# The second attention layer's first head: values turned to token rows by transposing transfers instead of TensorE transposes

## The chip, the cores and the metric

The kernel runs on one core of a Trainium2 chip. The metric is the device time of one execution in microseconds (us), as the median of several runs. Engines are named as the profile names them: PE is TensorE's matmul, PEld its weight load, DVE VectorE, ACT ScalarE, POOL GpSimd, SP the engine that issues most transfers. Each engine takes its instructions strictly in the order of its queue.

## What is computed

A two-layer trunk over 528 tokens (16 learned meta tokens and 512 real ones), width 1024, in float32. Layer one is gated linear attention; layer two is differential softmax attention with 8 heads:

```python
def diff_branch(xn, w_in, lam_vecs, gnorm, w_out, rel_table, lambda_init):
    proj = xn @ w_in
    q, k, v, z = jnp.split(proj, 4, axis=-1)          # per head: 2x128 q, 2x128 k, 256 v, 256 z
    ...
        s = jnp.einsum('bhpqd,bhpkd->bhpqk', qb, kh) * scale + bias[None, :, None]
        s = jnp.where(dist >= 0, s, -jnp.inf)
        p = jax.nn.softmax(s, axis=-1)
        a = p[:, :, 0] - lam * p[:, :, 1]
        return jnp.einsum('bhqk,bhkv->bhqv', a, vh)
    ...
    o = head_rms(o) * gnorm.astype(f32) * (1.0 - lambda_init)
    y = jax.nn.silu(z.astype(f32)) * o.reshape(B, L, D_INNER)
    return (y.astype(xn.dtype) @ w_out)
```

A final RMSNorm follows and the meta positions are dropped. What matters here: the value projection `v` comes out with channels on the partitions and tokens along the free axis, and the product of the attention weights with `v` needs tokens on the partitions. So `v` of every head has to be turned.

## The kernel before

**Precision.** Each float32 operand is split into a high and a low part (`split`: ACT writes the rounded high part, DVE subtracts it and writes the low one), and a product takes three matmul passes. Weights arrive by SP in `raw` (two buffers of 1 MB), ACT and DVE split them into `wh`/`wl`, `a11h`/`a11l` and so on, and PE consumes these. Most projections run as a `Unit`: a block product with seven instead of eight sub-products (p1 to p7), whose weight sums (`sum`, `raw<-raw,sum`, L360) are made by DVE. A unit's first product leaves its result in the PSUM bank `bx`; ACT copies it out (`partial`, L446, tile `u`), and only then may p6 add to the same bank.

**Order.** PE's order is the order in which the program issues its instructions. For the layer's steps a `Weaver` decides it: `fill` interleaves projection work with attention steps by estimated microseconds, `defer` runs a function after so much work, `follow` does the same for chains of steps. DVE, ACT and the transfers are placed by the framework's scheduler, with priorities (`urgent`, `soon`); after that each queue is fixed.

**Around the change.** At the end of layer one the program projects z and then v of head 0 of layer two (`z0r` in tile `x6`, `v0` in tile `x5`, stored back to front so that real tokens run from 511 down to 0 and the meta tokens from 15 to 0 stand in the last 16 columns). Then come, in this order on PE, q of head 0 (L415, banks `bv` and `by`), k of head 0 (L415, `bx` pair, then `bv`/`by`), the z projection of head 1 as a unit (L425, p1 in `bx`, p2 in `by`, p6 in `bx`), and inside it the first scores (L394). Beside this DVE and ACT make the sums of x that the units need (`token_sums2`, L1515 and the splits of `x4` to `x7`), split q and k, and split weights.

**How v is turned before.** `turned_back2(s, m, vt, first=True)` is called for m = 0 and 1. Each defers `post`: four 128x128 TensorE transposes into one PSUM bank (L856) and one of the last 32 columns (L857), then the splits into `s.v` (two tiles, tokens x 4 blocks x 256 channels) and `s.vm` (the meta tokens).

**How v of heads 1 to 6 is turned.** `turn_by_dma`: `leave` (called for each half m) has ACT rearrange the 32-bit words into two planes of 16-bit words (L583, tile `planes`) and issue a transfer to a DRAM buffer `vd` (L584). When both halves have left, `turn` is put on the list `behind` and issued on SP right after the next weight load: two transposing transfers into `planes` (L592) and one of 128 rows into `lands` for the meta tokens (L594). Later `done` splits `planes` into `s.v` (ACT L569, DVE L570) and `rest` splits the meta rows out of `lands` (L401, L402, L406). `tick` is a small DVE memset that keeps `done` behind a chosen instruction.

## Time and profile before

| | before |
|---|---|
| runs, us | 981.64, 981.70, 983.57; median 981.70 |
| the profiled execution, us | 980.58 |
| its span (first to last instruction), us | 978.8 |
| PE busy | 965.6 us, 99% of the span |
| DVE busy | 777.6 us, 79% |
| ACT busy | 621.5 us, 63% |
| mean granted TensorE clock | 0.999 of full speed |
| value splits of heads 1 to 6 from `planes` | L569 and L570, 12 instructions each |

Times in the trace are us from the span's start. "SPq" and "ACTq" rows are issues of transfers, not engine work. A matmul's row covers its pipeline, so neighbouring matmuls overlap; the distance between starts is what each costs. The stretch that the change touches lies between 478 us (end of v0's projection) and 530 us, in a program of 979 us.

### The profile page before, as it was taken

The page shows a single profiled execution, that of the slowest core. Times are in us where ns is not written, and L with a number is a line of the kernel's source. Part 1 is how long each engine was busy: PE and PEld are TensorE (multiplying, and loading weights), DVE is VectorE, ACT ScalarE, POOL GpSimd, SP SyncE. Part 2 cuts the span into 40 slices and gives each one's busy share as a digit, 9 for nine tenths or more (in the row PEclk, how much of TensorE's full clock was granted, in tenths as well). Part 3 has the DMA queues.
Part 4 walks back from the last instruction along what each step waited for, and adds up shares of the span by engine and source line. Part 5 has one row for each costly group of instructions (what it writes and reads, how often), then busy time and mean ns, then how long its engine had stood idle before and what let it go on. Part 6 is the DMA issues. An engine that isn't in the chain of part 4 may idle for free.

```text
span 978.8 us, 18153 instructions
## 1 busy us (share of the span) xinstructions
PE 965.6 (99%) x7049; PEld 913.2 (93%) x7049; DVE 777.6 (79%) x1584; ACT 621.5 (63%) x1310; POOL 50.3 (5%) x68
## 2 busy tenths in 40 slices
PE   9999999999999999999999999999999999999997
PEld 8999999999999999998999998899998999989996
DVE  7889885887888797566997985977968879677785
ACT  8775755567647556545757774576764667655573
POOL 1000000000000100000001001001010000000001
PEclk9999999999999999999999999999999999999999
DMA  7322224625363122212323424134252351612212
GB/s 195 87 85 62 77 72 136 146 94 130 120 153 114 59 87 87 72 59 87 98 87 95 139 75 148 54 98 137 86 147 86 94 141 47 186 57 86 87 65 86
DMA packets 113226, 98.37 MB, mean 100 GB/s; under 512 B 37341, under 2 KB 99069, under 8 KB 113136
## 3 DMA queue, kind: packets, MB, share of 16 engines
q1 hardware_dynamic: 109680, 90.66, 32.1%
q10 hardware_dynamic: 3456, 6.51, 1.9%
q8 instruction: 57, 0.93, 0.4%
q14 instruction: 33, 0.27, 0.1%
HBM read 83.64 MB, written 8.62 MB: 94 GB/s over the span
## 4 chain that ended last, share of the span: by engine, by line
PE 88%; DVE 2%; ACT 1%; issue 0%; POOLq 0%; ACTq 0%
PE bx L425 19%; PE bv L425 12%; PE bx L415 10%; PE by L425 10%; PE ps L394 9%; PE bx L962 5%; PE bx L394 3%; PE bv L962 2%; PE by L962 2%; PE by L394 2%; PE bv L394 2%; PE ps L1200 2%; PE by L415 1%; PE bv L415 1%; PE ps L1792 1%; PE bx L1792 1%
## 5 line engine op out<-in xcount | busy, mean ns | idle before, releaser
L274 DVE TENSOR_TENSOR wl<-raw,wh 128x1024 fp32r<-128x1024 f32 x98 | 119.6, 1222 | 23.4 <-ACT wh L273 16.2
L273 ACT ACTIVATE wh<-raw 128x1024 fp32r<-128x1024 f32 x98 | 103.1, 1054 | 53.5 <-PE by L962 24.7
L425 PE MATMUL bv<-x,wh 128*128 128x264 f32 (+1 forms) x656 | 97.9, 287 | 0.6 <-DVE z L473 0.6
L425 PE MATMUL bx<-x,wh 128*128 128x264 f32 (+1 forms) x640 | 95.2, 286 | 1.8 <-ACT u L446 1.5
L425 PEld LDWEIGHTS bv<-x,wh 128*128 128x128 f32 x656 | 86.4, 189 | 1.5 <-DVE z L473 0.9
L425 PEld LDWEIGHTS bx<-x,wh 128*128 128x128 f32 x640 | 84.5, 188 | 3.2 <-ACT u L446 2.4
L446 ACT ACTIVATE u<-bx 128x264 f32<-128x264 f32 (+1 forms) x120 | 45.5, 380 | 28.1 <-PE bx L425 24.4
L415 PE MATMUL bx<-x,wh 128*128 128x512 f32 (+1 forms) x256 | 62.6, 386 | 0.0
L274 DVE TENSOR_TENSOR wl<-sum,wh 128x1024 fp32r<-128x1024 f32 x41 | 50.1, 1222 | 15.2 <-ACT wh L273 14.6
L1715 POOL TENSOR_TENSOR st<-st,mhalf 128x1 f32<-128x1 f32 x32 | 31.5, 984 | 465.4 <-ACT on L1713 447.1
L425 PE MATMUL bv<-x,wl 128*128 128x264 f32 (+1 forms) x328 | 55.2, 285 | 0.1
L425 PE MATMUL bx<-x,wl 128*128 128x264 f32 (+1 forms) x320 | 54.0, 285 | 0.0
L1679 ACT ACTIVATE p<-p,st 128x528 f32<-128x528 f32 (+3 forms) x64 | 36.4, 569 | 24.6 <-DVE st L1677 24.1
L415 PEld LDWEIGHTS bx<-x,wh 128*128 128x128 f32 x256 | 44.5, 188 | 8.0
L273 ACT ACTIVATE wh<-sum 128x1024 fp32r<-128x1024 f32 x41 | 43.3, 1055 | 9.5 <-PE bv L425 3.4
L273 ACT ACTIVATE a11h<-raw 128x512 fp32r<-128x512 f32 x41 | 25.7, 628 | 35.5 <-DMA raw<-in_diff_w_in_dram 16.0
L425 PE MATMUL by<-x,a12h 128*128 128x264 f32 (+1 forms) x320 | 46.5, 285 | 0.0
L425 PE MATMUL bx<-x,a11h 128*128 128x264 f32 (+1 forms) x320 | 46.3, 285 | 0.0
L425 PEld LDWEIGHTS bv<-x,wl 128*128 128x128 f32 x328 | 45.9, 188 | 0.4 <-issue 0.3
L425 PEld LDWEIGHTS bx<-x,wl 128*128 128x128 f32 x320 | 45.2, 188 | 0.8 <-DVE wl L274 0.5
L425 PEld LDWEIGHTS bx<-x,a11h 128*128 128x128 f32 x320 | 42.2, 188 | 0.7
L425 PEld LDWEIGHTS by<-x,a12h 128*128 128x128 f32 x320 | 41.7, 188 | 0.0
(483 smaller groups left out, 2641.7 us busy)
## 6 DMA issues: line engine op xcount, KB each, us to landing
raw<-in_gla_w_in_dram SPq DMA_DIRECT2D x48, 512.0 KB, 4.1
raw<-in_diff_w_in_dram SPq DMA_DIRECT2D x42, 512.0 KB, 4.2
raw<-in_diff_w_in_dram SPq DMA_DIRECT2D x11, 1024.0 KB, 5.8
raw<-in_gla_w_out_dram SPq DMA_DIRECT2D x8, 1024.0 KB, 5.1
raw<-in_diff_w_out_dram SPq DMA_DIRECT2D x8, 1024.0 KB, 5.9
vd<-planes ACTq DMA_DIRECT2D x12, 268.0 KB, 2.5
vd<-keep ACTq DMA_DIRECT2D x8, 264.0 KB, 2.6
T<-bdr SPq DMA_DIRECT2D x8, 264.0 KB, 3.5
```

The lines of the kernel that those rows point to most:

```text
L273: act.activation(hi, src, AF.Copy)
L274: dve.tensor_tensor(lo, src, hi.bitcast(F32), op=ALU.subtract)
L394: pe.matmul(ps, l, r, start=first and n == 0, stop=last and n == 2, **kw)
L415: pe.matmul(bank, a[:, k, :], b[k] if n0 is None else b[k][:, n0 + i * nn:n0 + (i + 1) * nn], start=n == 0 and ks[0] == 0, stop=n == len(t ...
L425: pe.matmul(bank[:, :x[q].shape[2]], w[p][:, k * P:(k + 1) * P], x[q][:, k, :], start=first and i == 0, stop=i == len(PASSES) - 1, skip_gr ...
L446: W.moved = act.activation(t, self.bx[:, :self.n], AF.Copy, scale=self.sc)
L962: pe.matmul(banks[i][:, :HT], h.t[p][:, k, mm * P:(mm + 1) * P], s.y[q][k][:, i * HT:(i + 1) * HT], start=n == 0, stop=n == len(PASSES) - 1)
L1200: pe.matmul(o, s.kd[:, i, kc], s.qs[:, i, t0:t0 + n], start=i == 0, stop=i == 1)
L1679: act.activation(p[:, :nk], p[:, :nk], AF.Exp, scale=-1.0, bias=st[:, m:m + 1], accum_out=st[:, 2 + m:3 + m])
L1715: pool.tensor_tensor(ms, ms, mhalf[:, :1], op=ALU.pow)
L1792: pe.matmul(ps[i], yp[hd][p][:, k, b * P:(b + 1) * P], wt[q][cs.start // 512][:, 2 * hd + k, cs.start % 512:(cs.stop - 1) % 512 + 1], star ...
```

## The change

Head 0's values now take the road of heads 1 to 6. The call for m = 0 makes a `turn_by_dma` object with its own `planes` tile of 2 x 528 words; both calls `leave` at once. Two arguments are new: `ahead` (how much work lies between the second `leave` and the appearance of `turn` on the list; 3.0 instead of 4.0) and `at` (which rows of `lands` hold the meta tokens: row 96, since here the last 128 columns are read and the meta tokens come last).

```diff
-    def turn_by_dma(planes, groups, ends, us, done, last):
+    def turn_by_dma(planes, groups, ends, us, done, last, at=0, ahead=4.0):
...
-                W.follow((4.0, lambda: behind.append((turn, None))))
+                W.follow((ahead, lambda: behind.append((turn, None))))
...
-                last(lands[0][:32, 0, :])
+                last(lands[0][at:at + 32, 0, :])
...
-        if first or s is heads[-1]:
-            W.defer(2.2 if first else 1.4, post)
+        if s is heads[-1]:
+            W.defer(1.4, post)
+        elif first:
+            if m == 0:
+                s.leave = turn_by_dma(T(ep, [P, 2, L], F32, "planes", bufs=1),
+                                      [(slice(3, 1, -1), 0), (slice(1, None, -1), 2 * P)], L - P, 3.0, done, last, 96, 3.0)
+            s.leave(m, vt)
```

On PE the ten transposes (two times L856 x4 and L857) between the 12th and the 13th matmul of q's first half are gone, and nothing else in its order differs. On SP the three transposing transfers stand behind the two loads of `raw_1571`, the weights of head 1's z unit, and ahead of the next two loads. DVE gets the small memset of `tick` earlier, ahead of v0's projection. Otherwise ACT's and DVE's queues differ only from the end of v0's projection to about 527 us of the trace before, in head 0's second turn of the attention weights; behind that they are the same as before. Buffer numbers at the end of names differ between the two programs; the first number tells the tile.

ACT, first place: from the high parts of q and of the x sums (`x4` to `x7`) to those of head 1's z weights (`a11h`, `a12h`, `a22h`). Before:

```order
L273 ACTIVATE v0_1536_8777<-ps_1548_8817 128x4x128
L273 ACTIVATE x4_1551_8833<-hT_8_90 128x4x8
L273 ACTIVATE wh_1556_8854<-raw_1555_8852 128x1024
L273 ACTIVATE a11h_1573_9033<-raw_1571_9027 128x512
L276 ACTIVATE q0_1558_8858<-bv_1540_8782 128x512
L273 ACTIVATE a12h_1578_9045<-raw_1571_9027 128x512
L273 ACTIVATE a22h_1582_9054<-raw_1571_9027 128x512
```

Now, the same place further on in the queue:

```order
L276 ACTIVATE q0_1557_8844<-by_1559_8848 128x512
L569 ACTIVATE v0_1536_8777<-planes_1539_8780,tick_1560_8868 128x4x128 x2
L401 ACTIVATE vm_1538_8779<-lands_1554_8838,short_146 32x256
L402 ACTIVATE vm_1538_8779<-lands_1554_8838,short_146 32x256
L273 ACTIVATE x6_1551_8817<-hT_8_90 128x4x8
L273 ACTIVATE x7_1552_8818<-hT_8_90 128x4x256
L273 ACTIVATE a11h_1573_9028<-raw_1571_9022 128x512
L273 ACTIVATE a12h_1578_9040<-raw_1571_9022 128x512
L273 ACTIVATE a22h_1582_9049<-raw_1571_9022 128x512
```

The value splits moved from the front of q's splits to behind the second of them, and `x7` and the three weight splits now stand behind the value splits.

ACT, second place: the end of k's projection (`t`, `k0`) and the copy `u` out of `bx` in head 1's z unit. Before:

```order
L1643 ACTIVATE t_1566_8900<-by_1570_8966 128x264
L273 ACTIVATE wh_1580_9050<-raw_1571_9027 128x1024
L273 ACTIVATE k0_1563_8897<-t_1566_8900 128x512
L446 ACTIVATE u_1589_9082<-bx_1585_9061 128x256
L273 ACTIVATE k0_1563_8897<-t_1566_8900 128x16
```

Now:

```order
L1648 ACTIVATE t_1566_8890<-by_1570_8961 128x264
L273 ACTIVATE k0_1563_8887<-t_1566_8890 128x512
L273 ACTIVATE k0_1563_8887<-t_1566_8890 128x16
L273 ACTIVATE wh_1580_9045<-raw_1571_9022 128x1024
L446 ACTIVATE u_1589_9077<-bx_1585_9056 128x256
```

The weight split `wh_1580`, which reads the last weight sum that DVE makes in `raw_1571`, was two rows ahead of `u` and is now right ahead of it, behind k's splits.

DVE: from the low part of q's second half to the last weight sum (`raw<-raw,sum`). Before, the rows right behind q's second half:

```order
L277 SCALAR_TENSOR_TENSOR q1_1559_8859<-by_1560_8862,q0_1558_8858 128x512
L277 SCALAR_TENSOR_TENSOR x5_1552_8834<-hT_8_90,x5_1552_8834 128x4x256
L277 SCALAR_TENSOR_TENSOR x5_1552_8834<-hT_8_90,x5_1552_8834 128x4x8
L274 TENSOR_TENSOR x6_1553_8835<-hT_8_90,x6_1553_8835 128x4x8
L1515 TENSOR_TENSOR hT_8_90<-hT_8_90 128x4x256
L1515 TENSOR_TENSOR hT_8_90<-hT_8_90 128x4x8
L360 TENSOR_TENSOR sum_1575_9037<-raw_1571_9027 128x512
```

Now:

```order
L277 SCALAR_TENSOR_TENSOR q1_1558_8845<-by_1559_8848,q0_1557_8844 128x512
L570 TENSOR_TENSOR v1_1537_8778<-planes_1539_8780,v0_1536_8777 128x4x128
L277 SCALAR_TENSOR_TENSOR x5_1550_8816<-hT_8_90,x5_1550_8816 128x4x8
L570 TENSOR_TENSOR v1_1537_8778<-planes_1539_8780,v0_1536_8777 128x4x128
L406 SCALAR_TENSOR_TENSOR vm_1538_8779<-lands_1554_8838,short_146,vm_1538_8779 32x256
L274 TENSOR_TENSOR x6_1551_8817<-hT_8_90,x6_1551_8817 128x4x256
L274 TENSOR_TENSOR x6_1551_8817<-hT_8_90,x6_1551_8817 128x4x8
L1515 TENSOR_TENSOR hT_8_90<-hT_8_90 128x4x8
L274 TENSOR_TENSOR x7_1552_8818<-hT_8_90,x7_1552_8818 128x4x256
L274 TENSOR_TENSOR x7_1552_8818<-hT_8_90,x7_1552_8818 128x4x8
L274 TENSOR_TENSOR a11l_1574_9029<-raw_1571_9022,a11h_1573_9028 128x512
```

The three value instructions moved from ahead of q's first half to behind its second half; `x6`, `a11l` moved from ahead of them to behind them, and `x5`'s large part and one large L1515 moved to ahead of q's second half.

## The prediction

> **What bounds the kernel now.** I read the page's busy times and its chain first, then the chain of waits in order of time and the busy times by windows around the change, and last the timelines of each engine there.

> ```profile
> PE 965.6 (99%) x7049; PEld 913.2 (93%) x7049; DVE 777.6 (79%) x1584; ACT 621.5 (63%) x1310; POOL 50.3 (5%) x68
> PE 88%; DVE 2%; ACT 1%; issue 0%; POOLq 0%; ACTq 0%
> ```

> TensorE is busy for 99% of the span and 88% of the chain that ended last is TensorE's. The chain in order of time shows what the transposes cost on it:

> ```profile
> 478.25 2.78 PE bv L415 x12
> 481.03 0.44 PE ps L856 x4
> 481.57 0.44 PE ps L856 x4
> 482.12 2.79 PE bv L415 x12
> 484.91 5.61 PE by L415 x24
> ```

> q's first half (`bv`, 24 matmuls) takes from 478.25 to 484.91, 6.66 us, with the transposes inside; its second half (`by`, the same 24) takes 5.61. The ten transposes thus cost **1.05 us of the chain**. What stands beside TensorE there, by windows:

> ```profile
> core 0: us, PE busy (x) PEld busy (x) DVE busy (x) ACT busy (x) POOL busy (x), PEclk, DMA share, GB/s
> 480.00:490.00 10.00, 10.00 (x50) 8.20 (x49) 9.73 (x18) 8.84 (x18) 0.00 (x0) 1.00 0.40 122
> 490.00:500.00 10.00, 10.00 (x83) 9.91 (x82) 10.00 (x17) 5.00 (x12) 0.00 (x0) 1.00 0.34 107
> 500.00:510.00 10.00, 10.00 (x87) 10.00 (x85) 9.68 (x23) 5.85 (x14) 0.00 (x0) 1.00 0.32 105
> 486.00:492.00 6.00, 6.00 (x34) 5.14 (x33) 6.00 (x9) 4.61 (x8) 0.00 (x0) 1.00 0.00 0
> ```

> The reader is to see three things: TensorE has no hole here that the change could close beyond its own transposes; DVE has no room either (9.7 to 10 of 10 us), so whatever makes DVE wait comes out later; ACT has about 5 us of room in 490 to 500, and from 486 to 492 no transfer runs (share 0.00).

> **The change, part by part.** *Removed from PE:* the 1.05 us. It is all on the chain; without a new wait the end comes 1.05 us earlier.

> *ACT and DVE work.* The durations of the same steps for later heads:

> ```profile
> L583 ACT ACTIVATE planes<-t x12: 1079/1082/1098, 529.4 to 839.3; 128x1072 uint16<-128x1072 uint16 x12
> L569 ACT ACTIVATE v<-planes,tick x12: 707/710/727, 558.3 to 878.7; 128x512 fp32r<-128x512 f32 x12
> L570 DVE TENSOR_TENSOR v<-planes,v x12: 677/685/689, 560.3 to 881.9; 128x512 fp32r<-128x512 f32 x12
> L406 DVE SCALAR_TENSOR_TENSOR vm<-lands,short,vm x1: 474/474/474, 561.7 to 561.7; 32x256 fp32r<-32x256 f32 x1
> DMA to landing us min/median/max: 2.3/2.5/2.8
> ```

> ACT gains two rearrangements of 1.08 us; its splits change from PSUM to `planes` at about the same price. So some 2 us more on ACT, inside its room. DVE trades splits for splits (0.69 us each), a wash. The work itself costs nothing; what can cost is the waiting of ACT and DVE in order behind the transfers.

> *When the transfers land.* ACT's and SP's rows before:

> ```profile
> 479.35 1.32 ACT L1557 ACTIVATE x<-x,dgs 128x512 f32<-128x512 f32 x2
> 480.25 0.92 SPq L295 DMA_DIRECT2D raw<-in_diff_w_in_dram  x2
> 492.21 0.92 SPq L295 DMA_DIRECT2D raw<-in_diff_w_in_dram  x2
> ```

> By the new order ACT does the two rearrangements where L1557 stood (479.35 to 481.4), then L1557, and issues both transfers to `vd` at about 482.1 to 482.5. They need 2.3 to 2.8 us (last row of the fence above), and the weight load issued at 480.25 is moving at the same time (until about 485, since the share is 0.00 from 486). I take `vd` landed at 485 to 486.5. SP waits for that, then issues the transposing transfers; behind them in SP's queue stands only the load that was issued at 492.21, so it isn't held back. How long they take, from another head with little beside them:

> ```profile
> 719.90 2.59 SPq L592 DMA_TRANSPOSE planes<-vd  x2
> 722.54 1.25 SPq L594 DMA_TRANSPOSE lands<-vd  x1
> 721.00:722.50 1.50, 1.50 (x14) 1.50 (x14) 1.11 (x3) 1.50 (x5) 0.00 (x0) 1.00 0.81 167
> 722.50:723.00 0.50, 0.50 (x4) 0.40 (x3) 0.41 (x2) 0.47 (x4) 0.00 (x0) 1.00 0.54 62
> 723.00:724.50 1.50, 1.50 (x8) 1.18 (x7) 1.50 (x3) 0.69 (x3) 1.27 (x1) 1.00 1.03 180
> 724.50:725.00 0.50, 0.50 (x4) 0.40 (x3) 0.26 (x1) 0.40 (x2) 0.06 (x1) 1.00 0.59 56
> ```

> Two bursts with a dip after each: the second of the two ends some 4.7 us after the first issue; with the signal I take 5. So `planes` is there at **490 to 491.5**, `lands` a good microsecond later.

> *When the queues reach the value splits.* ACT stands before L569 once q's second half is split; q's last matmul ends at 490.52 - 1.05 = 489.5 (the chain's `by` row: 484.91 + 5.61), so ACT is there at about 490.2. DVE's rows:

> ```profile
> 492.10 0.68 DVE L277 SCALAR_TENSOR_TENSOR q<-by,q 128x512 fp32r<-128x512 f32 x1
> 492.70 1.32 DVE L277 SCALAR_TENSOR_TENSOR x<-hT,x 128x1024 fp32r<-128x1024 f32 x2
> 495.27 0.68 DVE L360 TENSOR_TENSOR sum<-raw 128x512 f32<-128x512 f32 x1
> 495.87 0.68 DVE L274 TENSOR_TENSOR a12l<-raw,a12h 128x512 fp32r<-128x512 f32 x1
> 501.41 0.69 DVE L360 TENSOR_TENSOR raw<-raw,sum 128x512 f32<-128x512 f32 x1
> ```

> A 512-wide step costs DVE 0.60 us (495.27 to 495.87), a 1024-wide one 1.14 by the same reckoning. DVE left q's second half at 492.7; ahead of that point the new order has one 512-wide split, two value splits and one meta pair less (2.4 us) and 1.14 us more of x sums; it waits 0.6 us for the later L1557, where before 0.27 us of 480 to 490 were idle (9.73 of 10), so 0.3 more. It gets to L570 at about **491.7**, or 0.7 us after ACT's L569 starts if that is later: with `planes` at 490 to 491.5, at 491.7 to 492.2.

> *Who waits for that.* Behind L570 on DVE stand `x6`, `x7`, `a11l`, k's low part and all weight sums down to `raw<-raw,sum`. That last row came 9.35 us after q's split (492.70 to the end of 501.41's step, 502.05). In the new order the stretch from L570 to it has two value splits (1.2), the meta rows (0.45), `x6` (1.14) and `a11l` (0.60) more, and `x5` and one L1515 (1.14 each) less: 10.4 us. I add 0.3 for ACT's meta rows, which DVE meets. DVE is through at 502.4 to 502.9. Then ACT:

> ```profile
> 502.68 1.07 ACT L273 ACTIVATE wh<-raw 128x1024 fp32r<-128x1024 f32 x1
> 503.63 0.63 ACT L273 ACTIVATE k<-t 128x512 fp32r<-128x512 f32 x1
> 504.15 0.39 ACT L446 ACTIVATE u<-bx 128x256 f32<-128x256 f32 x1
> 504.87 0.87 PE L425 MATMUL bx<-x,wh 128*128 128x256 f32 x6
> 521.61 1.57 PE L394 MATMUL ps<-v,aT 128*128 128x256 f32 x12
> ```

> In the new order `wh` (0.95 as a step) waits for that sum and `u` (0.39) stands right behind it; PE's p6 (504.87) may not add to `bx` before `u` is out. `u` ends at 502.4 + 0.95 + 0.4 = 503.8 to 504.3. PE, 1.05 us early, wants p6 at 503.8. Before, `u` ended at 504.54, 0.33 us ahead of p6. So p6 is **late by 0 to 0.5 us**, and from there each microsecond of delay at L570 is one on the chain. The other waits have more room: the values themselves are needed only at 521.61, `a11h` about 6 us after it is made; k's low part has about 1 us.

> *Sum.* Gain 1.05 minus 0.25 (middle of 0 to 0.5) = 0.8 us. The profiled execution took 980.58 (span 978.8), so its counterpart would take 979.8; the median of the runs is 1.1 us above that execution, so the median goes from 981.7 to **980.9**. From the second turn of head 0's attention weights on the orders agree, so nothing else moves.

> [...] The trace has nobody wait for the values before 521.61, which is why I weigh the queues' wait and not the transfers' length.

> **The rivals.** 0.2% is 1.96 us here, about what a measurement of this kernel can tell from no change.

> *1, the forecast: gain kept, less at most 0.5 us;* 980.65 to 981.2. For it: no transfer runs from 486 to 492, and TensorE has no other wait. Chance 0.53; of this 0.06 would be read as over 0.2% faster, by the scatter of the runs alone (981.64 to 983.57).

> *2, gain eaten.* `planes` at 491.5 to 494: p6 is late by 0.5 to 3 us, and the time is 981.2 to 983.6, in the middle 982. For it: where a load was issued right ahead, the pair's issue alone took longer:

> ```profile
> 536.46 4.28 SPq L592 DMA_TRANSPOSE planes<-vd  x2
> 843.92 6.04 SPq L592 DMA_TRANSPOSE planes<-vd  x2
> ```

> That is 1.7 us more than 2.59, so `planes` at 492.5 and p6 1.3 us late. Against it: these had their load half a microsecond ahead, here it is 5 us. Chance 0.32, of it 0.03 over 0.2%.

> *3, slower: DVE and ACT stand in front of the transfers.* If `vd` is held to 486.5 by the weight load and the pair is as slow as at 843.92 (3.45 us more), `planes` comes at 495, DVE starts L570 at 495.7, and p6 is 4 us late: 981.7 - 1.05 + 4 = 984.6. It decides from `planes` at 494 on (3 us lost, 1.05 won). [...] Chance 0.15, of it 0.12 over 0.2%.

> A gain over 1.96 us would need holes in TensorE that the windows don't show. That the transfers aren't used is out: the order has them, and the transposes are gone.

> **How the numbers follow.** The time is rival 1's, 980.9. The range 980.0 to 983.4 holds rivals 1 and 2 and leaves 0.2 out: scatter below (0.06) and rival 3 above with the end of rival 2. Faster 0.06; slower 0.03 + 0.12 = 0.15; within 0.2% the rest, 0.79.

> **What would show it.** Right: q's two halves both 5.6 us; `planes` split by ACT at 490 to 491.5 with little idle time before; `raw<-raw,sum` at about 502; `u` ending within 0.5 us of p6's start. Wrong: idle time of ACT ahead of L569 and of DVE ahead of L570 above 1.5 us with L1515, x sums and k's low part pushed out, and PE waiting for ACT's `u` (L446) or for DVE's k ahead of the scores (L394); or a PE hole behind 505 that has another releaser.

## The result, and the profile after

The changed kernel takes 987.62 us in the median (986.93 to 987.80), the kernel before, timed beside it, 981.64; the ratio is 1.0059, 95% interval 1.0047 to 1.007. It is some 6 us slower. The forecast was 980.9 with a range to 983.4, so it was wrong in size and in sign. The profiled execution took 987.65 us with a span of 985.6, 6.8 more than the span before; 0.65 of this is there ahead of the change (q starts at 478.74 instead of 478.09).

The page's busy times; TensorE does 10 matmuls fewer and idles more:

```profile
span 985.6 us, 18136 instructions
PE 966.0 (98%) x7039; PEld 912.3 (93%) x7039; DVE 777.4 (79%) x1584; ACT 623.8 (63%) x1310; POOL 51.8 (5%) x68
```

TensorE's timeline from q to the first scores (start, duration, what, and in brackets the idle time before it and who ended it):

```profile
478.74 3.87 PE L415 MATMUL bv<-x,wh 128*128 128x512 f32 x16
...
484.30 3.90 PE L415 MATMUL by<-x,wh 128*128 128x512 f32 x16
...
502.53 0.63 PE L425 MATMUL bx<-x,a11l 128*128 128x256 f32 x4
504.99 1.40 PE L425 MATMUL by<-x,a12h 128*128 128x256 f32 x8 [1.83 <-ACT t L1648]
506.19 1.05 PE L425 MATMUL by<-x,a12l 128*128 128x256 f32 x4
507.65 1.65 PE L425 MATMUL bx<-x,wh 128*128 128x256 f32 x6 [0.41 <-ACT u L446]
509.10 1.68 PE L394 MATMUL ps<-k,q 128*128 128x264 f32 x12
```

The kernel before has its first scores here:

```profile
505.58 1.61 PE L394 MATMUL ps<-k,q 128*128 128x264 f32 x12
```

q's first half takes 5.56 us instead of 6.66: the gain is there, 1.1 us. Then TensorE stands still twice, 1.83 and 0.41 us, and the matmuls behind the first stand are slow: p6 takes 1.65 us where it took 0.87. Against the kernel before TensorE was 0.45 us early at 482 us and is 3.52 us late at the scores (509.10 against 505.58), so this stretch costs 3.97 us. From the start of q's first half to the scores it is 30.36 us instead of 27.49, a net loss of 2.87. The windows over it (the column behind POOL is the granted clock):

```profile
504.00:506.00 2.00, 1.01 (x8) 1.01 (x9) 2.00 (x3) 1.67 (x5) 0.00 (x0) 0.96 0.00 0
506.00:508.00 2.00, 1.59 (x7) 1.30 (x7) 1.97 (x6) 1.73 (x3) 0.00 (x0) 0.50 0.00 0
508.00:510.00 2.00, 2.00 (x13) 2.00 (x13) 1.98 (x4) 0.64 (x2) 0.00 (x0) 0.69 0.05 9
```

The clock is halved from about 505.8 to 509.2: 2 us times (0.04 + 0.50 + 0.31) are 1.70 us of full speed lost. The two stands are 2.24 us; together 3.94. The sum fits, but its terms aren't independent prices: p6 may start only when `u` is out, at 507.60 (last ACT row below), however fast the matmuls ahead of it run. Section 7 has an execution without this fall of the clock in which the scores come as late.

Why TensorE stands: the timelines of SyncE's queue, of ScalarE and its queue (ACTq), and of VectorE.

```profile
480.90 0.92 SPq L295 DMA_DIRECT2D raw<-in_diff_w_in_dram  x2
488.63 2.61 SPq L592 DMA_TRANSPOSE planes<-vd  x2
...
482.07 0.82 ACTq L584 DMA_DIRECT2D vd<-planes  x2
...
494.18 1.34 ACT L569 ACTIVATE v<-planes,tick 128x512 fp32r<-128x512 f32 x2 [3.33 <-DMA planes<-vd]
...
503.32 1.06 ACT L273 ACTIVATE wh<-sum 128x1024 fp32r<-128x1024 f32 x1 [2.55 <-DVE sum L360]
...
504.55 0.38 ACT L1648 ACTIVATE t<-by 128x264 f32<-128x264 f32 x1
...
507.24 0.36 ACT L446 ACTIVATE u<-bx 128x256 f32<-128x256 f32 x1
...
494.93 0.69 DVE L570 TENSOR_TENSOR v<-planes,v 128x512 fp32r<-128x512 f32 x1 [2.70 <-ACT v L569]
```

The planes' two writes were issued by 482.9, but the transposes that wait for them start only at 488.63. ScalarE then stands 3.33 us in front of the value splits and VectorE 2.70; VectorE's weight sums come late by that much; ScalarE waits for a sum (2.55 us), and right behind stands the copy of k's second half out of the bank `by`. TensorE's p2 (a12h) writes into that bank, and so it waits.

Behind the scores the lag grows from 3.5 to 7.1 us at the end, in small steps and one large one near 900 us, although behind about 527 us the rows on all queues are the same as before. The load of that place (two transfers of 512 KB) in the kernel before and after (SyncE's issue, VectorE's first sum of it, and, after, TensorE):

```profile
892.39 1.22 SPq L295 DMA_DIRECT2D raw<-in_diff_w_in_dram  x2
...
898.02 0.69 DVE L360 TENSOR_TENSOR sum<-raw 128x512 f32<-128x512 f32 x1 [3.00 <-DMA raw<-in_diff_w_in_dram]
```

```profile
897.87 0.92 SPq L295 DMA_DIRECT2D raw<-in_diff_w_in_dram  x2
...
905.09 0.69 DVE L360 TENSOR_TENSOR sum<-raw 128x512 f32<-128x512 f32 x1 [4.59 <-DMA raw<-in_diff_w_in_dram]
...
908.97 0.75 PE L394 MATMUL ps<-v,aT 128*128 128x256 f32 x4 [1.14 <-DVE aT L274]
```

From issue to sum it is 5.63 us before and 7.22 after, and then TensorE waits 1.14 us.

### The profile page after: what moved, and what is told of

The parts are those of the page before. It is cut to its first block, busy times and chain, and to the rows that moved or that the text cites. A ratio compares the mean times of both kernels' runs of the same rounds, so it can differ in the third digit from the quotient of the medians.

```text
span 985.6 us, 18136 instructions
## 1 busy us (share of the span) xinstructions
PE 966.0 (98%) x7039; PEld 912.3 (93%) x7039; DVE 777.4 (79%) x1584; ACT 623.8 (63%) x1310; POOL 51.8 (5%) x68
## 5 line engine op out<-in xcount | busy, mean ns | idle before, releaser
L274 DVE TENSOR_TENSOR wl<-raw,wh 128x1024 fp32r<-128x1024 f32 x98 | 119.7, 1223 | 23.8 <-ACT wh L273 16.4
L273 ACT ACTIVATE wh<-raw 128x1024 fp32r<-128x1024 f32 x98 | 103.1, 1054 | 52.7 <-PE by L962 24.5
L425 PE MATMUL bx<-x,wh 128*128 128x264 f32 (+1 forms) x640 | 96.2, 288 | 2.9 <-ACT u L446 2.2
L425 PE MATMUL bv<-x,wh 128*128 128x264 f32 (+1 forms) x656 | 97.9, 287 | 0.8 <-DVE z L473 0.7
L425 PEld LDWEIGHTS bx<-x,wh 128*128 128x128 f32 x640 | 85.1, 190 | 4.8 <-ACT u L446 3.2
L425 PEld LDWEIGHTS bv<-x,wh 128*128 128x128 f32 x656 | 86.5, 189 | 1.6 <-DVE z L473 0.9
L446 ACT ACTIVATE u<-bx 128x264 f32<-128x264 f32 (+1 forms) x120 | 45.5, 380 | 29.5 <-PE bx L425 26.0
L415 PE MATMUL bx<-x,wh 128*128 128x512 f32 (+1 forms) x256 | 62.5, 386 | 0.0
L274 DVE TENSOR_TENSOR wl<-sum,wh 128x1024 fp32r<-128x1024 f32 x41 | 50.1, 1223 | 15.1 <-ACT wh L273 14.6
L425 PE MATMUL bv<-x,wl 128*128 128x264 f32 (+1 forms) x328 | 55.1, 285 | 0.1
L425 PE MATMUL bx<-x,wl 128*128 128x264 f32 (+1 forms) x320 | 54.0, 285 | 0.1
L415 PEld LDWEIGHTS bx<-x,wh 128*128 128x128 f32 x256 | 44.5, 188 | 8.0
L273 ACT ACTIVATE wh<-sum 128x1024 fp32r<-128x1024 f32 x41 | 43.3, 1055 | 11.7 <-PE bv L425 3.5
L273 ACT ACTIVATE a11h<-raw 128x512 fp32r<-128x512 f32 x41 | 25.7, 628 | 36.1 <-DMA raw<-in_diff_w_in_dram 16.3
L425 PE MATMUL by<-x,a12h 128*128 128x264 f32 (+1 forms) x320 | 46.8, 286 | 1.8 <-ACT t L1648 1.8
L425 PE MATMUL bx<-x,a11h 128*128 128x264 f32 (+1 forms) x320 | 46.3, 285 | 0.0
L425 PEld LDWEIGHTS bv<-x,wl 128*128 128x128 f32 x328 | 45.9, 188 | 0.4 <-issue 0.3
L425 PEld LDWEIGHTS bx<-x,wl 128*128 128x128 f32 x320 | 45.2, 188 | 0.9 <-DVE wl L274 0.7
L425 PEld LDWEIGHTS by<-x,a12h 128*128 128x128 f32 x320 | 41.8, 189 | 2.1 <-ACT t L1648 2.0
L425 PEld LDWEIGHTS bx<-x,a11h 128*128 128x128 f32 x320 | 42.2, 188 | 0.7
```

What stands on the lines that cost most here:

```text
L273: act.activation(hi, src, AF.Copy)
L274: dve.tensor_tensor(lo, src, hi.bitcast(F32), op=ALU.subtract)
L415: pe.matmul(bank, a[:, k, :], b[k] if n0 is None else b[k][:, n0 + i * nn:n0 + (i + 1) * nn], start=n == 0 and ks[0] == 0, stop=n == len(t ...
L425: pe.matmul(bank[:, :x[q].shape[2]], w[p][:, k * P:(k + 1) * P], x[q][:, k, :], start=first and i == 0, stop=i == len(PASSES) - 1, skip_gr ...
L446: W.moved = act.activation(t, self.bx[:, :self.n], AF.Copy, scale=self.sc)
```

## The experiments

Theory A: the planes' write lands late, ScalarE and VectorE stand at the splits, and TensorE pays. B: the order of ScalarE's row costs the wait by itself. C: the transfers slow other transfers, the wait is a symptom. Times are medians; ratios are to the kernel before, timed beside it (981.5 to 981.8 us), with their 95% intervals.

**1. The splits later in the queues** (the delay 3.0 of `turn_by_dma` raised).

```diff
-  [...], L - P, 3.0, done, last, 96, 3.0)
+  [...], L - P, 16.0, done, last, 96, 3.0)     (and 28.0)
```

> As the run with 28.0, with a delay of 16.0: the splits stand behind the next tiles of the weights' sums, a few rows later than in the changed kernel. Theory A: the first split comes to its place at about 495 us, after the planes have landed (491.3 to 494), so most of the standing still is gone; 981 to 984.5 us. Rival B: 985 us or more. Rival C: 986 to 988 us.

> Edit: in the changed kernel the two value splits of head 0 are queued later (the delay before them 28.0 instead of 3.0), so that ScalarE and VectorE reach them just ahead of the second transposed scores; the transfers stay where they are. Theory A (the transfers land late and ScalarE and VectorE, which run in order, stand still at the splits): the 3.33 us at L569 and 2.70 us at L570 go, TensorE's 1.83 us wait for ScalarE's copy goes, and the stage keeps its gain of 1.1 us; the local part of the loss (4.1 of the 6.0 us) goes and the time is 980.5 to 983.6 us, the upper end if what was lost further on stays. Rival B (the order of the row alone, the key copy behind the weight sums, costs the wait whatever the transfers do): TensorE still waits 1 us or more before a12h, 985 us or more. Rival C (the extra transfers slow other transfers, the wait is only a symptom): 986 to 988 us.

With 16.0: 983.20 us, ratio 1.0013 (1.0005 to 1.0022). The first split comes at 493.40 with 0.41 us of wait, and TensorE runs through:

```profile
502.04 0.63 PE L425 MATMUL bx<-x,a11l 128*128 128x256 f32 x4
502.51 1.11 PE L425 MATMUL by<-x,a12h 128*128 128x256 f32 x8
...
503.93 0.87 PE L425 MATMUL bx<-x,wh 128*128 128x256 f32 x6
504.63 1.64 PE L394 MATMUL ps<-k,q 128*128 128x264 f32 x12
```

The scores start 0.95 us earlier than before the change, 26.39 us behind the start of q's first half (27.49 before): A stands here, B falls (the copy still follows a `wh` that waits for VectorE). With 28.0: 988.03 us, ratio 1.0066 (1.0053 to 1.0078). A's number was missed, not its mechanism. The early stretch is clean here too, but now the values themselves are late, a price that I hadn't put in (TensorE's timeline, then the clock behind it by windows):

```profile
523.43 0.38 PE L394 MATMUL ps<-v,aT 128*128 128x256 f32 x1 [2.51 <-ACT v L569]
524.67 1.72 PE L394 MATMUL ps<-v,aT 128*128 128x256 f32 x11 [0.86 <-DVE v L570]
```

```profile
526.00:528.00 2.00, 2.00 (x11) 2.00 (x11) 0.45 (x1) 0.65 (x3) 0.54 (x1) 0.50 0.00 0
```

**2. The cause of the late landing.** The next head's gate-weight load (two transfers of 512 KB, not one), which ran beside the planes' write, is kept behind the transposes on SyncE's queue; near the change no other row moves.

```diff
+            i = sp.dma_start(...)          # in load_blocks
+            if w is d_w_in and c0 == 6400:
+                tc.keep_in_program_order(i)
```

> The changed kernel, with the load of the next head's gate weights (512 KB), which ran beside the planes' write, kept behind the three transposing transfers on SyncE's queue; nothing else moves. Theory A with its cause (the write of the planes lands late because that load runs beside it): the write lands 2.3 to 3.0 us after its issue instead of 5.7, the transposes are issued at 485 to 486 us instead of 488.6, the planes are there by 490 us, and ScalarE's 3.33 us at L569 fall to under 1 us; the load itself lands at about 493 to 494 us. The time is then set by whether the sums of that load are late: 983 to 987 us. If the write is slow by itself: still 5 us or more, and with the load behind it 988 to 990 us.

983.08 us, ratio 1.0016 (1.0007 to 1.0025). Its timelines:

```profile
482.79 0.82 ACTq L586 DMA_DIRECT2D vd<-planes  x2
...
485.88 2.61 SPq L594 DMA_TRANSPOSE planes<-vd  x2
...
489.89 3.40 SPq L295 DMA_DIRECT2D raw<-in_diff_w_in_dram  x4
...
491.47 1.33 ACT L571 ACTIVATE v<-planes,tick 128x512 fp32r<-128x512 f32 x2
```

From the start of the write's issue to the transposes' 3.1 us instead of 6.6; ScalarE doesn't wait for the planes, and TensorE doesn't wait before a12h: the scores come 26.45 us behind the start of q's first half, 1.04 earlier than before the change. That the load delayed the write is thus shown, and with it A. The load's own later landing costs nothing up to there.

**3. The two sides by themselves:** the transposes left out without any transfer (the splits read values that aren't turned), and the transfers added to the kernel before with nobody reading them.

```diff
-            pt, pm = to_tokens(vt, RBLK if first else HBLK, vt[:, end - 32:end])
+            if first:
+                pt, pm = vt[:, :512], vt[:32, :P]
+            else:
+                pt, pm = to_tokens(vt, HBLK, vt[:, end - 32:end])
```

> The kernel before with the ten transposes of the values of head 0 left out: the splits read the values as they stand, without being turned, so the output is another; no transfer is added. It prices what the change takes away. All theories: TensorE is 1.05 us shorter between the halves of q, and the time falls by 0.8 to 1.2 us, to about 980.6 us. If TensorE's gain there is given back by the next wait, 981.6 us.

> The kernel before, with the ten transposes on TensorE kept, plus the added plane copies, writes and transposing transfers of the change, whose result nobody reads. It prices the transfers without the wait for them. Theory A: only the two plane copies on ScalarE (0.7 us each) and the later landing of the next weights can show: 981.6 to 982.6 us. Rival C: the loss of 5 to 6 us is here too, 985.5 to 988 us.

Transfers alone: 982.79 us, ratio 1.0012 (1.0003 to 1.002), far from C's 985.5 and a little over A's 982.6. The transposes left out: **983.46 us, ratio 1.0015 (1.0006 to 1.0024): slower with less work**, which no theory had. q's first half is 5.57 us there and the scores come after 26.39, so the gain is made; but the load near 900 us is slow (6.94 us, TensorE waits 0.86), and the clock is halved from 693.8 to 697.2, behind TensorE's wait for `u` near 690. Both come with no transfer added. (This profile is of the slowest execution of eleven, 986.49 us; its clock was also halved from 7.74 to 14.56 us, at the program's start. Rows of ScalarE and VectorE between 480 and 528 us stand in another order.)

**4. Where the packets of instructions fall (theory D).** The page's queue table of the kernel before has a queue for instructions:

```profile
q8 instruction: 57, 0.93, 0.4%
```

These are 57 packets of 16 KB for 7049 matmuls and as many weight loads, one for every 124 of each. From these counts I took them for TensorE's code, as an estimate: the table names no engine. If that holds, twenty instructions fewer move each later packet. The kernel before, with six wide warm-up matmuls in place of eleven at 15 to 18 us (each is two records in the trace, so twenty instructions fewer with the weight loads) and nothing else changed but one small row of VectorE at 28 us:

```diff
-   warm_up((3, 3, 1, 4)[2 * n + i], idle)
+   warm_wide(((384,), (384,), (128,), (256, 128, 128))[2 * n + i], idle)
```

> The kernel before, its values still turned on TensorE and no transfer added; alone eleven warm-up matmuls at 15 to 18 us on TensorE, whose result nobody reads, are written as six wider ones over the same columns, so that TensorE's program has some twenty instructions fewer ahead of the second layer, as in the changed kernel. It tests a theory that the runs so far suggest (D): TensorE's instructions come in packets of 16 KB through the same transfer engines, the place of each packet is set by the count of instructions before it, and twenty fewer move a packet into the weight load near 900 us, which then lands 1.4 us later. D: the load near 900 us lands 5.4 to 5.6 us after its issue instead of 4.1, TensorE waits 0.9 to 1.1 us there, the gap near 690 us is 1.75 instead of 1.55 us; the time is 982.3 to 983.8 us. Rival E (those losses come from the earlier place of TensorE's work or from the transfers): nothing changes there, 981.3 to 982.2 us.

983.71 us, ratio 1.0027 (1.0015 to 1.004). TensorE's rows lie within 0.2 us of the kernel before up to 690 us, and then:

```profile
892.47 0.92 SPq L295 DMA_DIRECT2D raw<-in_diff_w_in_dram  x2
...
899.59 0.69 DVE L360 TENSOR_TENSOR sum<-raw 128x512 f32<-128x512 f32 x1 [4.49 <-DMA raw<-in_diff_w_in_dram]
...
903.48 0.75 PE L394 MATMUL ps<-v,aT 128*128 128x256 f32 x4 [1.06 <-DVE aT L274]
```

These are D's numbers: 7.12 us from issue to sum, a wait of 1.06, a gap of 1.73 near 690; the two transfers land 5.6 us after their issue instead of 4.1. In the changed kernel the packet there, seen in the transfers from 900.0 to 900.5 us, takes 21.5% of what 16 transfer engines have in that time, so 1.72 us of one. The end of the same load is then a trickle, by windows:

```profile
q8 instruction: 1, 0.02, 21.5%
```

```profile
901.50:903.00 1.50, 1.50 (x14) 1.50 (x14) 0.00 (x0) 0.75 (x4) 0.55 (x1) 1.00 1.03 349
903.37:904.87 1.50, 1.50 (x13) 1.28 (x12) 0.00 (x0) 1.13 (x2) 0.00 (x0) 1.00 0.07 23
```

The last two columns are the DMA share and GB/s: for its last 1.5 us the load moves at a share of 0.07, about one transfer engine of 16. That this is the engine which had the packet is my reading; the table doesn't name it.

The other direction, as many instructions more at the program's start, on the run with 16.0:

```diff
-    warm_up(10)
+    for c in [P] * 5 + [P // 2] * 10:
+        pe.matmul(warm[:, :c], ones, ones[:, :c], start=True, stop=True)
```

> The run with the delay of 16.0, and five of the ten warm-up matmuls at the program's start written as ten of half the width, so that TensorE has twenty instructions more there, as many as the change takes away later. Theory D: from the second layer on the packets of instructions stand where they stood before the change; the load near 900 us lands in 4.1 us, TensorE's wait of 0.9 us there goes, and the gain of 0.9 to 1.0 us of the missing transposes is kept: 980.6 to 981.6 us, about 2 us under the run with 16.0 alone. Rival E: 982.6 to 983.6 us, as without the warm-up's change.

> The run with the delay of 16.0 and twenty more instructions at the start once more, for one look at whether its late weight load at 790 us (which landed 2 us later than elsewhere) comes again: theory D says the same places again, so the same wait near 817 us; if it was chance, the time is about 981 us.

983.29 us, ratio 1.0023 (1.0012 to 1.0034): D's time was missed. In its profile the packet comes ahead of the load and the wait is gone, but another load, issued at 789.95, is late and costs 1.1 us by 817. The second profiled execution (982.43 us) loses 0.6 us there, and has the packet near 900 behind the load's issue, 7.21 us, a wait of 1.14. So the places aren't fixed by the count alone.

The 18 profiled executions fall into two groups at this place. Packet 0.3 us before to 0.3 us after the load's issue: the sum starts 5.4 to 6.0 us after the issue and TensorE doesn't wait (9 of them, the kernel before's three among them). Packet 2.4 to 3.4 us after it: 6.9 to 7.2 us, and a wait of 0.8 to 1.1 us (9, the changed kernel's three among them). With the trickle this shows that the packet sets the load's landing. The count sets the packet's place in most of them: all eight executions with 7039 matmuls have it late, eight of the nine with 7049 have it early (the second one above is the ninth), and the run of section 5, with 7043, has it early.

**5. The halved clock.** Two fp32 matmuls, unread, in the place of TensorE's first stand.

```diff
             def p2():
+                if W.busy:
+                    t = ps_tile()
+                    for _ in range(W.busy):
+                        pe.matmul(t, ones, ones[:, 0:1].to_broadcast([P, 512]), start=True, stop=True)
...
+            W.busy = 2
```

> The changed kernel, with two matmuls of 512 columns in fp32 (some 0.85 us each), whose result nobody reads, on TensorE in front of a12h, where it stands idle for 1.83 us. The planner moves some rows of ScalarE and VectorE behind that place. If the half clock from 505.6 to 509.6 us (1.71 us lost) is set off by that idle time: the granted clock stays at 1.00 there and the time falls by 1.2 to 1.8 us, to 985.8 to 986.4 us. If the clock falls for another reason: 987.3 to 988.5 us.

984.74 us, ratio 1.0043 (1.0029 to 1.0057), by the ratios 1.6 us less than the changed kernel. The clock stays at 1.00 (timeline, then windows):

```profile
502.69 1.88 PE L481 MATMUL ps<-ones 128*128 128x512 f32 x4
505.15 1.21 PE L425 MATMUL by<-x,a12h 128*128 128x256 f32 x8 [0.58 <-ACT t L1654]
```

```profile
506.00:508.00 2.00, 1.02 (x9) 0.82 (x8) 1.97 (x6) 1.57 (x3) 0.00 (x0) 1.00 0.00 0
```

Both expected ranges were missed, because the packet near 900 us came ahead of the load here, too (5.52 us), and rows of VectorE moved. So the time doesn't give the fall's price. The timeline does: the scores come 30.20 us behind the start of q's first half, where they came after 30.36, so without the fall all but 0.2 us of the local loss stays.

**6. The same count of instructions again, at the change's own place:** ten of q's matmuls written as two halves each, for three kernels.

```diff
+                if W.halve and n > 13:
+                    for h in range(2):
+                        pe.matmul(bank[:, h], a[:, k, :], b[k][:, h], start=False, stop=h == 1 and n == len(todo) - 1)
+                    continue
...
+                W.halve = not hd and i == 0
```

> The changed kernel, with ten of the 24 matmuls of q's first half (where the ten transposes stood) written as two of 256 columns each, so that TensorE again has as many instructions there as before the change; the planner moves a few rows of VectorE and ScalarE some 15 us later. Theory A (the wait for the splits) says that the stage from 494 to 510 us loses what it lost in the changed kernel; theory D (places of the packets of instructions) that the packet near 900 us comes 0.2 to 0.5 us ahead of the weight load's issue again, the sums start 5.5 us after it instead of 7.2, and TensorE's 1.1 us wait there goes. Together 985.5 to 986.8 us. If only the wait for the splits matters: 987.3 to 988 us.

> The run with the delay of 16.0, with the same ten matmuls split in two. Theories A and D together: no wait before a12h, no wait near 900 us, the gap near 690 us back at 1.5 to 1.6 us, and of the gain of 1.0 us what the ten extra weight loads leave: 980.6 to 981.5 us, at or a little under the kernel before. If the places of the packets don't matter: 983.0 to 983.6 us, as without the split.

> The run in which the weight load stands behind the transposing transfers, with the same ten matmuls split in two. Theories A and D together: 980.6 to 981.6 us; if the places of the packets don't matter: 982.8 to 983.4 us, as without the split.

On the changed kernel: 984.15 us, ratio 1.0036 (1.0023 to 1.0049), by the ratios 2.3 us less, and below the expectation; TensorE waits 2.00 and 0.98 us, so A's wait is there, the load near 900 us takes 5.51, and the clock was not halved in its profile. On the run with 16.0: 982.22, ratio 1.0006 (0.9996 to 1.0015), 0.7 over what was expected; 290 and 817 us cost it waits that the profile before doesn't have (but two further profiles of the kernel before, in section 7, have one or both). On the run with the load behind the transposes: **980.62 us, ratio 0.9987 (0.9978 to 0.9995)**, faster than both kernels, and as expected. Here TensorE doesn't wait near 505 or 900 us (it does, 0.62 us, near 817):

```profile
893.69 1.20 SPq L295 DMA_DIRECT2D raw<-in_diff_w_in_dram  x2
...
899.17 0.69 DVE L363 TENSOR_TENSOR sum<-raw 128x512 f32<-128x512 f32 x1 [2.85 <-DMA raw<-in_diff_w_in_dram]
```

**7. Kernel or chance:** the two kernels themselves, profiled again.

> The changed kernel itself, a second profiled execution. If the half clock belongs to the wait: granted clock 0.5 for 3.4 us from about 505 us again, and 987 to 988 us. If it is chance: a look without it, 985.5 to 986.3 us. The packet of TensorE's instructions near 900 us: 2.2 to 3.0 us behind the load's issue, sums 7.0 to 7.2 us after it, if its place belongs to the kernel.

> The changed kernel itself, a third profiled execution: as the second.

> The kernel before, a second profiled execution. If the packet's place belongs to the kernel: 0.25 to 0.5 us ahead of the load's issue near 892 us, sums 5.5 us after it, no wait of TensorE there, 980.5 to 982 us. If it is chance: a look in which it comes behind, with 1.0 to 1.2 us of wait, 982 to 983.5 us.

> The kernel before, a third profiled execution: as the second.

987.34, 985.96, 982.70 and 981.72 us. The wait before a12h is in every profiled execution of the changed kernel (1.83, 2.41, 2.18 us), as is the slow load near 900 (7.22, 6.99, 6.88). The halved clock is there once in each, but not at one place: at 505 us in the first and third, and in the second behind the wait for `u` near 694, with 2.41 us of wait before a12h and no fall. Which wait halves the clock depends on where it lies against a fixed grid of time, as the last section shows. What the fall costs depends on the place, too. From the start of q's first half to the scores the three take 30.36, 30.30 and 30.43 us: the one without the fall is no faster by more than 0.13 us, since p6 waits for `u` in any case (its second stand is 0.98 us instead of 0.41). Near 694 no later wait hides it, and the fall adds 1.6 us to the lag. The kernel before shows neither in three executions (27.49 us to the scores in each); it varies at 290 and 817 us instead, by 1.0 us at 290 in the second and by 0.5 to 0.6 at 817 in the second and third.

## Why the prediction was wrong

The step that failed is the landing of `vd`, a term that was sized too small; behind it came a term that was put at nothing, the places of the instruction packets. The ratios make a sum: the changed kernel 1.0059, without the wait for the planes 1.0016, with the count of instructions restored as well 0.9987. Of +5.8 us, the wait with what follows from it is 4.2 (3.91 of it up to the scores, 30.36 against 26.45), the restored count 2.9 (with a few rows of VectorE and ScalarE that the scheduler moved), and what is left is a gain of 1.3. The 2.9 belongs to that one kernel: the same ten split matmuls were worth 2.3 us on the changed kernel and 0.7 on the one with 16.0, where the two intervals overlap.

- *The gain of 1.05 us* was right: 1.1 us on the chain, and 1.3 (0.5 to 2.2) in the kernel that keeps it.
- *"I take `vd` landed at 485 to 486.5"* is the first step that failed. It was near 488.5, 6.56 us behind the first issue where the prediction allowed 4.4 at most. The sentence before it named the load that was moving at the same time, and still allowed only 1.6 us more than the 2.3 to 2.8 us that such writes take for later heads. The load's two transfers of 512 KB and the planes' two of 264 KB together finished late; with the load behind, the planes' write had landed before 485.9, 3.1 us after its issue.
- *Planes at 490 to 491.5* failed with it: the splits start at 494.18 (ScalarE) and 494.93 (VectorE instead of 491.7). That is rival 3's case, given 0.15: planes at 495, p6 4 us late. The stretch lost 3.97 us. The chain behind it was right: from the first L570 to the end of `raw<-raw,sum` VectorE took 11.3 us (10.7 in the prediction), and `u` was out 1.36 us later (1.35). With the planes on time (section 2) the scores came 1.04 us early, as the prediction has them.
- *"TensorE has no other wait"* failed. The chain through `u` to p6 was followed, but not ScalarE's copy of k's second half, which stands behind a `wh` that waits for VectorE's sum and holds the bank `by` that p2 needs. 1.83 us of the 2.24 were there. It is a stand that the prediction didn't see, but it adds nothing to its price: `u` was out at 507.60 and p6 started at 507.65, so without the stand at p2 TensorE would have stood longer at p6.
- *The clock* was no term of the sum. Up to the scores it need not be one: with and without the fall they come within 0.13 us of each other. Near 690 us the fall costs 1.5 to 1.6 us where it comes (the changed kernel's second profile, and those of the run with 16.0 and of section 2).
- *"nothing else moves"* failed too: no row moved, but instructions were taken out, and the instruction packets moved against the loads. In the nine executions with the late packet TensorE's lag against the first profile of the kernel before grows by 1.3 to 1.6 us around 900 us, in the others by 0.4 at most, so this place alone takes more than the change could win. Kernels without any added transfer lose time, too: the run without the transposes (+1.6 us) and the kernel before with other warm-up matmuls (+2.2). How the rest of the 2.9 us splits between the stand near 690 us, the clock behind it and the moved rows isn't shown.
- *"I weigh the queues' wait and not the transfers' length"* held: with the load out of the way (section 2) nobody waited for the transfers, and ScalarE's splits start at 491.47 with no wait for the planes. The fastest kernel here uses them, but only with the ten matmuls split as well; without that it is at 1.0016.

What stays open: which instruction asks for a packet, and why two executions of one kernel place it differently; the smaller steps of the changed kernel's lag, 0.65, 0.46 and 0.25 us behind 534, 678 and 690 us of the trace before, are not told apart one by one; and I did not try whether another place of the packets alone makes the kernel before faster.

## What to carry to other kernels

A transfer's time from a quiet place didn't hold here beside a load: the planes' write, put at 2.3 to 2.8 us from later heads, was followed by the transposes 6.6 us after its issue with the load beside it, and 3.1 us after with the load behind. So read the share of the window that it will really run in, and if a load is there that isn't urgent, queue it behind. Of an engine that will stand still, follow every row behind the stand, bank copies included, to whoever waits. And before a difference of a quarter per cent is put down to a change, see whether the count of instructions moved: writing unread warm-up matmuls as fewer, wider ones over the same columns cost 2.2 us, twice what this change was meant to win.

## What the runs showed of the hardware

```profile
503.82:507.23 3.41, 1.69 (x12) 1.48 (x12) 3.38 (x7) 2.81 (x6) 0.00 (x0) 1.00 0.00 0
507.23:510.64 3.41, 2.71 (x22) 2.71 (x23) 3.41 (x11) 1.69 (x4) 0.00 (x0) 1.00 0.11 19
691.55:694.97 3.42, 1.59 (x14) 1.38 (x13) 2.83 (x10) 3.37 (x8) 0.00 (x0) 1.00 0.31 107
694.97:698.38 3.41, 3.41 (x14) 3.41 (x14) 3.17 (x8) 1.50 (x5) 0.00 (x0) 0.50 0.00 0
```

- A 16 KB packet of the instruction queue near 900 us took 0.9 us with no load moving (the kernel before: 10.9% of 16 transfer engines from 892.0 to 892.5 us) and 1.2 to 1.7 us inside a load of two times 512 KB (15.5% from 895.0 to 895.5 in the run with wider warm-up matmuls, 21.5% in the changed kernel). In the run with wider warm-up matmuls, where the packet fell into it, the load landed 5.6 us after its issue; in the kernel before, 4.1.
- Ten matmuls of 512 columns written as twenty of 256 cost 0.1 us or less (q's first half takes 5.62 us with them and 5.56 without).
